# An encoder layer with a routed mixture of experts on one core: its last two experts, its final normalisation and its stores are reordered

## The chip, the cores and the metric

The kernel runs on one core of a Trainium2 chip. The metric is the device time of one execution, in microseconds (us). The engines are TensorE (PE in the profile, its weight loads PEld), VectorE (DVE), ScalarE (ACT), GpSimd (POOL) and SyncE (SP), whose queue issues all the loads and stores here. A small q behind an engine's name in a row (DVEq, SPq) means its sequencer, the part that takes in instructions, register loads, branches and waits.

## The reference

The input x has 256 positions of 2048 values, all float32. One layer adds a gated sum of a spatial-gating branch and a differential-attention branch to x, then adds a mixture of 16 experts, and a last norm follows. The part that the change touches is this:

```python
x = x + hier_moe(rmsnorm(x, norm2_g), ...)   # 16 SwiGLU experts, top 2 per position
out = rmsnorm(x, final_g)                    # x * rsqrt(mean(x*x) + 1e-6) * final_g
```

An expert has w1 and w3 of 2048 x 512 and w2 of 512 x 2048. Each position uses two experts of one group of four.

## The kernel before

The 256 positions are two token tiles t of 128 partitions. The experts are worked off in pairs, each expert with room for 64 positions (`CAP`), so that one pair's 128 positions fill the partitions. Positions beyond the room of 64 are handled at the very end by `rest()` (line 832), under a branch on the largest count (`most`, line 650). In the run that is profiled the branch is not taken.

**First stage of the experts** (lines 750 to 766): four rounds q of four experts. In each of eight steps b a round gathers two blocks of the positions' columns (`gather`, line 679) and multiplies them with four weight blocks of 1 MB (`stream.whole()`, line 57). `swiglu` (line 720) ends a round, and `turn` (line 732) transposes its result one round later. This stage reads 128 blocks.

**Second stage** (lines 807 to 829): for each of four column groups n of 512 and each of eight pairs p, two blocks of w2 (1 MB each) are multiplied into one PSUM bank `ps` (line 817). ScalarE writes the weighted sum's high part `yh` (line 826), VectorE the rest `yl` (line 827), and `back` (line 784) multiplies both with the matrix `PT` that puts the positions back, into the accumulator `ya`, one bank for each token tile (line 792). `back` runs one pair late, so that TensorE has the next pair's blocks in between; only the last call, on line 829, has nothing in between. `yh` and `yl` share a pool of two buffers, so a pair's `yh` waits until `back` has read the last pair's. The second stage reads 64 blocks.

**Final norm.** For n below 3, the last pair's `back` adds x, squares (line 797) and multiplies with the final norm's weights `gf` (`last_norm`, line 775) while the weights of the next n stream in. For n = 3, x is put into `ya` by an identity matmul (line 789); after the last pair ScalarE squares `ya` of both tiles (line 801), then copies it to `xf` (line 803). `last_scale` (line 779) makes the reciprocal root for each tile with a sum and a scaling on VectorE and a power on GpSimd (line 126). Lines 893 and 896 load the branch's register on each engine and branch. After it six instructions scale (lines 905 to 910) and six stores write 2 MB (line 913): columns 0 to 511, 512 to 1535 and 1536 to 2047, each for two tiles.

**What sets the order.** A scheduler puts each engine's instructions in a fixed order when the program is built; `issue_after(i)` holds what a block traces on i's engine behind i. Blocks go into 27 SBUF slots of 1 MB (`Slots`, line 30), of which 17 are free for the stream once the final norm's five are taken (line 770). Loads share eight completion semaphores in turn, so a load is issued only when the eighth before it has landed. `gf` is one load on line 771: it copies the one row of 2048 weights to all 128 partitions, 1 MB in all, and stands in SP's queue behind 17 of the second stage's blocks:

```python
xf, zf, gf = [slots.take()[0] for _ in range(2)], [slots.take()[0] for _ in range(2)], slots.take()[0]
nc.sync.dma_start(gf, rows(A["final_g"], D))            # 128 partitions, step 0
```

Of the kernel before, what the change touches and what calls it, by code (L numbers as in the profile page):

```python
# [22 lines left out]
NE = 16  # L23
CAP = 64
# [72 lines left out]
def encoder(ctx, tc, A, out, stop=None):  # L97
    nc = tc.nc
    V, SC, PE, GP = nc.vector, nc.scalar, nc.tensor, nc.gpsimd

    consts = ctx.enter_context(tc.tile_pool(name="consts", bufs=1))
# [407 lines left out]
    for i in range(4):  # L509
        if i % 2 == 0:  # L510
# [5 lines left out]
            for j in range(4):  # L516
                c = j % 2 * NK + (i + j // 2) * 4
# [16 lines left out]
    for n in range(4):  # L534
# [44 lines left out]
    for n in (0, 2):  # L579
        ps = acc(), acc()  # L580
# [139 lines left out]
    def swiglu(q, s13):  # L720

        out = []
        for p in range(2):
            g = wk(name="g")
            for j in range(2):
                h, ps = slice(j * CAP, (j + 1) * CAP), s13[p][:, j * 512:(j + 1) * 512]
                SC.activation(g[h], ps[:CAP], AF.Silu)  # L727
                V.tensor_tensor(g[h], g[h], ps[CAP:], op=OP.mult)  # L728
            out.append(g)
        return out  # L730

    def turn(q, gated):

        if q % 2 == 0:
            hids.append(slots.take())
        for p in range(2):
            f = bank("f")
            for j in range(4):
                PE.transpose(f[:, j * 128:(j + 1) * 128], gated[p][:, j * 128:(j + 1) * 128], ident)
            SC.copy(view(hids[-1], 4)[:, 2 * (q % 2) + p], f)  # L740

    hids, PTs = [], None
    gathering = gather()
    xg, last, scaled = next(gathering)
    with tc.issue_after(scaled):
        weigh()
    PTs = slots.take(F32R)
    PT = view(PTs, 8)
    gated = None
    for q in range(NE // 4):  # L750
        s13 = acc("s13"), acc("s13")
        for b in range(8):
            with tc.issue_after(last):
                if b == 1 and gated:
                    turn(q - 1, gated)
                xg_next, last, _ = next(gathering, (None, last, None))
            with tc.issue_after(last):
# [12 lines left out]
    xf, zf, gf = [slots.take()[0] for _ in range(2)], [slots.take()[0] for _ in range(2)], slots.take()[0]  # L770
    nc.sync.dma_start(gf, rows(A["final_g"], D))
    sf = consts.tile([128, 2, 4], F32, name="sf")
    rf = consts.tile([128, 2], F32, name="rf")

    def last_norm(n, t):
        c = slice(n * 512, (n + 1) * 512)
        V.tensor_tensor(zf[t][:, c], xf[t][:, c], gf[:, c], op=OP.mult)

    def last_scale(t):
        V.tensor_reduce(rf[:, t:t + 1], sf[:, t], axis=AX, op=OP.add)  # L780
        V.tensor_scalar(rf[:, t:t + 1], rf[:, t:t + 1], 1.0 / D, 1e-6, op0=OP.mult, op1=OP.add)
        rsqrt(rf[:, t:t + 1], rf[:, t:t + 1])

    def back(n, p, ya, ys):

        c = slice(n * 512, (n + 1) * 512)
        if p == 0 and n == 3:
            for t in range(2):
                PE.matmul(ya[:, t], ident, x1_cols(t, n), start=True, stop=False)
        for y in ys:  # L790
            for t in range(2):
                PE.matmul(ya[:, t], PT[:, p, t * 128:(t + 1) * 128], y, start=n < 3 and p == 0 and y is ys[0],  # L792
                          stop=p == NE // 2 - 1 and y is ys[1])
        if p == NE // 2 - 1 and n < 3:
            for t in range(2):
                V.tensor_tensor(xf[t][:, c], ya[:, t], x1_cols(t, n), op=OP.add)
                SC.activation(zf[t][:, c], xf[t][:, c], AF.Square, accum_out=sf[:, t, n:n + 1])
                last_norm(n, t)
        elif p == NE // 2 - 1:
            for t in range(2):  # L800
                SC.activation(xf[t][:, c], ya[:, t], AF.Square, accum_out=sf[:, t, n:n + 1])
            for t in range(2):
                SC.copy(xf[t][:, c], ya[:, t])


    waiting = None
    for n in range(4):
        ya = acc("y").rearrange("p (t n) -> p t n", t=2)
        for p in range(NE // 2):
            ps = bank("ye")  # L810
            with tc.issue_after(mm.ins):
                hid = view(hids[p // 4], 4)[:, p % 4].rearrange("p (k s) -> p k s", k=4)
                for b in range(2):
                    w = stream.whole().rearrange("p (j k n) -> p j k n", j=2, k=2)
                    for k in range(2):
                        for j in range(2):
                            mm = PE.matmul(ps[j * CAP:(j + 1) * CAP], hid[:, b * 2 + k, j * CAP:(j + 1) * CAP], w[:, j, k],  # L817
                                           start=b == 0 and k == 0, stop=b == 1 and k == 1)
# [9 lines left out]
            waiting = n, p, ya, (yh, yl)  # L828
    back(*waiting)


    def rest():
# [57 lines left out]
                        V.tensor_tensor(xf[t][:, c], ps[:, t * 512:(t + 1) * 512], xf[t][:, c], op=OP.add)  # L890

    slots.give(*hids, PTs)
    most_v = nc.values_load(most[0:1, 0:1], min_val=0, max_val=S)
    for t in range(2):
        last_scale(t)
    with tc.If(most_v > CAP):
        rest()
        for t in range(2):
            for n in range(4):
                SC.activation(bank("sq"), xf[t][:, n * 512:(n + 1) * 512], AF.Square, accum_out=sf[:, t, n:n + 1])  # L900
                if n < 3:
                    last_norm(n, t)
            last_scale(t)
    c0, c1, c2 = slice(0, 512), slice(512, 1536), slice(1536, D)
    V.tensor_scalar(zf[0][:, c0], zf[0][:, c0], rf[:, 0:1], None, op0=OP.mult)  # L905
    SC.activation(zf[1][:, c0], zf[1][:, c0], AF.Copy, scale=rf[:, 1:2])
    V.tensor_scalar(zf[0][:, c1], zf[0][:, c1], rf[:, 0:1], None, op0=OP.mult)
    SC.activation(zf[1][:, c1], zf[1][:, c1], AF.Copy, scale=rf[:, 1:2])
    for t in range(2):
        V.scalar_tensor_tensor(zf[t][:, c2], xf[t][:, c2], rf[:, t:t + 1], gf[:, c2], op0=OP.mult, op1=OP.mult)  # L910
    for c in (c0, c1, c2):
        for t in range(2):
            nc.sync.dma_start(out[0, t * 128:(t + 1) * 128, c], zf[t][:, c])

# [46 lines left out]
```

## Time and profile before

| | us |
|---|---|
| median of 3 runs | 1084.84 (1083.54 to 1085.14) |
| the profiled execution | 1083.54 |
| its span in the trace | 1081.6 |
| TensorE busy | 1048.3 (97% of the span) |
| VectorE busy | 510.0 (47%) |
| ScalarE busy | 395.9 (37%) |
| share of the load and store queue, over 16 DMA engines | 76.3% |

TensorE's share is an average over stages with different limits. The matmuls' ends are modelled, and they are pipelined, so a short wait between two of them does not show as idle. In the strip of 40 slices the DMA engines stand at 9 tenths and about 421 GB/s from slice 25 to the last but one, that is in all of the time of the two expert stages but their first few tens of us. All times in the rows are us from the start of the span; the time of an execution has 1.94 us more than its span.

### The profile page before, as it was taken

How to read it: one execution, taken by the hardware profiler on the slowest of the kernel's cores; microseconds unless marked ns; L12 is line 12 of the kernel's file. 1: busy time of each engine (PE TensorE's matmuls, PEld its weight loads, DVE VectorE, ACT ScalarE, POOL GpSimd, SP SyncE). 2: the span in 40 equal slices, each digit the busy share in tenths (PEclk: the TensorE clock that was granted, in tenths of full speed). 3: DMA queues.
4: the chain of work that ended last, by engine and by line, in shares of the span. 5: the costliest groups of instructions: out<-in, count | busy, mean ns of one | idle time of the engine just before them, and what ended most of it. 6: DMA issues, size and time to landing. Idle time of an engine off the chain costs nothing. (4 is left out here: it accounts for less than half of the span.)

```text
span 1081.6 us, 13529 instructions
## 1 busy us (share of the span) xinstructions
PE 1048.3 (97%) x5436; PEld 700.1 (65%) x5436; DVE 510.0 (47%) x745; ACT 395.9 (37%) x554; POOL 9.1 (1%) x16
## 2 busy tenths in 40 slices
PE   7999999999999999999999999999999998999995
PEld 7989988998788888888887743444434432333331
DVE  8775676866778655566655541312313111122121
ACT  7564555555566444444443320211211101111112
POOL 1000000000000000000000000000000000000000
PEclk9999999999999999999999999999999999999997
DMA  9914455455875656556964769999999999999994
GB/s 338 420 61 171 156 197 190 158 209 181 272 265 191 228 192 231 191 203 248 364 254 160 299 269 422 421 421 421 422 421 421 420 421 421 421 422 421 420 421 188
DMA packets 48642, 323.29 MB, mean 299 GB/s; under 512 B 5664, under 2 KB 5824, under 8 KB 11072
## 3 DMA queue, kind: packets, MB, share of 16 engines
q1 hardware_dynamic: 48576, 322.39, 76.3%
q8 instruction: 44, 0.72, 0.3%
q14 instruction: 22, 0.18, 0.0%
HBM read 320.25 MB, written 2.11 MB: 298 GB/s over the span
## 5 line engine op out<-in xcount | busy, mean ns | idle before, releaser
L280 PE MATMUL acc<-slot,slot 128*128 128x512 f32 x1920 | 445.2, 391 | 1.1 <-ACT slot L85 0.6
L280 PEld LDWEIGHTS acc<-slot,slot 128*128 128x128 f32 x1920 | 358.2, 188 | 75.2 <-DVE slot L86 1.0
L86 DVE TENSOR_TENSOR slot<-slot,slot 128x1024 fp32r<-128x1024 f32 (+1 forms) x210 | 253.9, 1211 | 166.0 <-ACT slot L85 165.0
L85 ACT CAST slot<-slot 128x1024 fp32r<-128x1024 f32 (+1 forms) x210 | 218.5, 1042 | 254.1 <-PE acc L280 182.1
L763 PE MATMUL s<-slot,slot 128*64 128x512 f32 x1024 | 228.3, 596 | 3.7 <-DMA slot<-in_w_dram 3.7
L763 PEld LDWEIGHTS s<-slot,slot 128*64 128x64 f32 x1024 | 70.1, 137 | 138.3 <-issue 118.5
L264 PE MATMUL acc<-slot,slot 128*128 128x256 f32 x1152 | 143.5, 286 | 6.0 <-ACT slot L85 5.9
L264 PEld LDWEIGHTS acc<-slot,slot 128*128 128x128 f32 x1152 | 140.8, 193 | 7.0 <-ACT slot L85 6.1
L817 PE MATMUL ye<-slot,slot 128*64 128x512 f32 x512 | 122.6, 604 | 4.7 <-DMA slot<-in_w_dram 3.6
L693 DVE TENSOR_TENSOR slot<-slot,slot 128x256 fp32r<-128x256 f32 x64 | 26.3, 419 | 136.8 <-PE gather L696 122.0
L817 PEld LDWEIGHTS ye<-slot,slot 128*64 128x64 f32 x512 | 31.6, 136 | 79.7 <-issue 39.4
L692 ACT CAST slot<-slot 128x256 fp32r<-128x256 f32 x64 | 25.6, 407 | 153.6 <-PE gather L696 143.6
L827 DVE SCALAR_TENSOR_TENSOR yl<-ye,slot_c,yh 128x512 fp32r<-128x512 f32 x32 | 24.0, 750 | 115.8 <-ACT yh L826 115.8
L826 ACT ACTIVATE yh<-ye,slot_c 128x512 fp32r<-128x512 f32 x32 | 22.0, 688 | 129.1 <-PE y L792 129.1
L696 PEld LDWEIGHTS gather<-slot 128*128 128x128 f32 x256 | 32.9, 189 | 19.8 <-issue 19.5
L700 DVE SCALAR_TENSOR_TENSOR slot<-gather,g,slot 128x256 f32<-128x256 f32 x64 | 27.9, 477 | 27.5 <-PE gather L696 27.3
L696 PE MATMUL gather<-slot 128*128 128x256 f32 x256 | 39.5, 296 | 0.0
L728 DVE TENSOR_TENSOR g<-g,s 64x512 f32<-64x512 f32 x16 | 11.1, 691 | 32.5 <-ACT g L727 32.4
L792 PEld LDWEIGHTS y<-yh,slot 128*128 128x128 f32 x64 | 9.6, 188 | 25.6 <-issue 24.8
L727 ACT ACTIVATE g<-s 64x512 f32<-64x512 f32 x16 | 9.5, 591 | 42.7 <-PE s L763 38.9
L792 PE MATMUL y<-yh,slot 128*128 128x512 f32 x64 | 23.7, 452 | 0.3 <-ACT yh L826 0.3
L792 PE MATMUL y<-yl,slot 128*128 128x512 f32 x64 | 20.2, 397 | 0.1
(191 smaller groups left out, 482.1 us busy)
## 6 DMA issues: line engine op xcount, KB each, us to landing
slot<-in_w_dram SPq DMA_DIRECT2D x192, 1024.0 KB, 19.8
slot<-in_w_in_dram SPq DMA_DIRECT2D x68, 1024.0 KB, 4.9
slot<-in_w_out_dram SPq DMA_DIRECT2D x16, 1024.0 KB, 5.0
slot<-in_w_proj_a_dram SPq DMA_DIRECT2D x8, 1024.0 KB, 4.9
slot<-in_w_proj_b_dram SPq DMA_DIRECT2D x8, 1024.0 KB, 4.8
slot<-in_w_in_dram SPq DMA_DIRECT2D x6, 512.0 KB, 8.1
slot<-in_xT_dram SPq DMA_DIRECT2D x8, 256.0 KB, 7.7
slot<-bias_rows SPq DMA_DIRECT2D x8, 256.0 KB, 6.3
```

The lines of the kernel that those rows point to most:

```text
L85: nc.scalar.copy(h, w)
L86: nc.vector.tensor_tensor(l, w, h.bitcast(F32), op=OP.subtract)
L264: PE.matmul(ps[:, j * S:(j + 1) * S], w[:, j * 128:(j + 1) * 128], v, start=kk == 0 and first and j % 2 == 0, stop=kk == nk - 1 and w is w ...
L280: PE.matmul(ps[:, t * 512:(t + 1) * 512], v[:, t * 128:(t + 1) * 128], w, start=kk == 0 and v is a and w is wh, stop=kk == nb * 4 - 1 and ...
L692: SC.copy(s[:, :, 0], x)
L693: V.tensor_tensor(s[:, :, 1], x, s[:, :, 0].bitcast(F32), op=OP.subtract)
L696: mm = PE.matmul(ps[:, k * S:(k + 1) * S], s[:, t, i], d[:, t], start=k == t == i == 0, stop=k == t == i == 1, skip_group_check=True)
L700: out = V.scalar_tensor_tensor(xg[:, k], ps[:, k * S:(k + 1) * S], g2[:, kk:kk + 1], r_row, op0=OP.mult, op1=OP.mult)
L763: mm = PE.matmul(ps[i * CAP:(i + 1) * CAP], xg[:, k, j * CAP:(j + 1) * CAP], w[:, i, k], start=b == k == 0, stop=b == 7 and k == 1)
L792: PE.matmul(ya[:, t], PT[:, p, t * 128:(t + 1) * 128], y, start=n < 3 and p == 0 and y is ys[0], stop=p == NE // 2 - 1 and y is ys[1])
L817: mm = PE.matmul(ps[j * CAP:(j + 1) * CAP], hid[:, b * 2 + k, j * CAP:(j + 1) * CAP], w[:, j, k], start=b == 0 and k == 0, stop=b == 1 and ...
L827: V.scalar_tensor_tensor(yl, ps, sc, yh.bitcast(F32), op0=OP.mult, op1=OP.subtract)
```

## The change

1. The load of `gf` to 128 partitions is gone. In round q = 3, before step b = 5, a new function `final_rows` takes three slots, loads the row of 8 KB to one partition, and four matmuls with a column of ones copy it to all partitions in PSUM; ScalarE copies the four banks to `gf`.
2. The largest count is copied to `beyond` after round q = 1, and each engine loads the branch's register from it ahead of the second stage.
3. For the last pair of the last column group the w2 matmuls run in two halves of 256 columns with a bank each, and `yh`, `yl` and `back` too.
4. `last_scale` treats both token tiles in one sum, scaling and power.
5. For n = 3 too, `last_norm` now multiplies with `gf` ahead of the branch, reading the accumulator in PSUM, beside ScalarE's copy of it.
6. After the branch VectorE scales tile 0 and ScalarE tile 1, in four pieces of 256, 512, 768 and 512 columns, and eight stores write them.

```diff
@@ swiglu
-                V.tensor_tensor(g[h], g[h], ps[CAP:], op=OP.mult)
+                done = V.tensor_tensor(g[h], g[h], ps[CAP:], op=OP.mult)
+        if q == 1:
+            with tc.issue_after(done.ins):
+                V.tensor_copy(beyond, most)
@@ ahead of the first stage
+    beyond = consts.tile([128, 1], I32, name="beyond")
+    def final_rows():
+        xf.extend(slots.take()[0] for _ in range(2))
+        gf.append(slots.take()[0])
+        row = xf[0][0:1, :]
+        nc.sync.dma_start(row, rows(A["final_g"], D, 1))
+        for n in range(4):
+            c, ps = slice(n * 512, (n + 1) * 512), bank("gf")
+            mm = PE.matmul(ps, ones[0:1, :], row[:, c], start=True, stop=True)
+            SC.copy(gf[0][:, c], ps)
+        return mm.ins
@@ first stage, for b in range(8): with tc.issue_after(last):
+                if q == 3 and b == 5:
+                    last = final_rows()
@@ after the first stage
-    xf, zf, gf = [slots.take()[0] for _ in range(2)], [slots.take()[0] for _ in range(2)], slots.take()[0]
-    nc.sync.dma_start(gf, rows(A["final_g"], D))
+    zf, gf = [slots.take()[0] for _ in range(2)], gf[0]
+    most_v = nc.values_load_multi_w_load_instructions(beyond[0:1, 0:1], min_val=0, max_val=S, bass_reorder=False)[1][0]
-    def last_scale(t):
-        V.tensor_reduce(rf[:, t:t + 1], sf[:, t], axis=AX, op=OP.add)
-        V.tensor_scalar(rf[:, t:t + 1], rf[:, t:t + 1], 1.0 / D, 1e-6, op0=OP.mult, op1=OP.add)
-        rsqrt(rf[:, t:t + 1], rf[:, t:t + 1])
+    def last_scale():
+        V.tensor_reduce(rf, sf, axis=AX, op=OP.add)
+        V.tensor_scalar(rf, rf, 1.0 / D, 1e-6, op0=OP.mult, op1=OP.add)
+        rsqrt(rf, rf)
@@ back, last pair, n = 3
             for t in range(2):
-                SC.activation(xf[t][:, c], ya[:, t], AF.Square, accum_out=sf[:, t, n:n + 1])
-            for t in range(2):
-                SC.copy(xf[t][:, c], ya[:, t])
+                SC.activation(zf[t][:, c], ya[:, t], AF.Square, accum_out=sf[:, t, n:n + 1])
@@ second stage
+                halves = [(ps, slice(0, 512))]
+                if n == 3 and p == NE // 2 - 1:
+                    halves = [(ps[:, :256], slice(0, 256)), (bank("ye")[:, :256], slice(256, 512))]
                 for b in range(2):
                     w = stream.whole().rearrange("p (j k n) -> p j k n", j=2, k=2)
+                    for ph, cy in halves:
...
-            SC.activation(yh, ps, AF.Copy, scale=sc)
-            V.scalar_tensor_tensor(yl, ps, sc, yh.bitcast(F32), op0=OP.mult, op1=OP.subtract)
+            for ph, cy in halves:
+                SC.activation(yh[:, cy], ph, AF.Copy, scale=sc)
+                V.scalar_tensor_tensor(yl[:, cy], ph, sc, yh[:, cy].bitcast(F32), op0=OP.mult, op1=OP.subtract)
+                ys += [(yh[:, cy], cy), (yl[:, cy], cy)]
@@ end
-    most_v = nc.values_load(most[0:1, 0:1], min_val=0, max_val=S)
+    last_scale()
     for t in range(2):
-        last_scale(t)
+        SC.copy(xf[t][:, 1536:], y3[:, t])
+        last_norm(3, t, y3[:, t])
     with tc.If(most_v > CAP):
         rest()
...
-    c0, c1, c2 = slice(0, 512), slice(512, 1536), slice(1536, D)
...
+    chunks = [slice(0, 256), slice(256, 768), slice(768, 1536), slice(1536, D)]
+    for c in chunks:
+        V.tensor_scalar(zf[0][:, c], zf[0][:, c], rf[:, 0:1], None, op0=OP.mult)
+        SC.activation(zf[1][:, c], zf[1][:, c], AF.Copy, scale=rf[:, 1:2])
         for t in range(2):
             nc.sync.dma_start(out[0, t * 128:(t + 1) * 128, c], zf[t][:, c])
```

## Rows read from the trace of the kernel before

**Rows 1.** Busy time by stretches, the line of columns first.

```profile
core 0: us, PE busy (x) PEld busy (x) DVE busy (x) ACT busy (x) POOL busy (x), PEclk, DMA share, GB/s
...
700.00:800.00 100.00, 100.00 (x514) 42.39 (x511) 21.93 (x61) 14.67 (x34) 0.00 (x0) 1.00 1.01 421
...
945.00:950.00 5.00, 2.52 (x13) 0.72 (x14) 0.75 (x1) 0.39 (x1) 0.00 (x0) 1.00 1.02 423
...
1020.00:1063.00 43.00, 42.88 (x178) 15.51 (x176) 8.67 (x13) 7.52 (x13) 0.00 (x0) 1.00 0.98 406
1063.00:1082.00 19.00, 5.61 (x24) 1.98 (x18) 4.32 (x10) 4.68 (x9) 1.10 (x2) 0.70 0.30 113
```

**Rows 2.** DMA issues of the whole run: count, KB each, us to landing.

```profile
slot<-in_w_dram SPq DMA_DIRECT2D x192, 1024.0 KB, 19.8
...
slot<-in_final_g_dram SPq DMA_DIRECT2D x1, 1024.0 KB, 19.8
```

**Rows 3.** SP's timeline from 780 us: start, us, instruction.

```profile
781.60 143.37 SPq L60 DMA_DIRECT2D slot<-in_w_dram  x58
927.14 0.33 SPq L771 DMA_DIRECT2D slot<-in_final_g_dram  x1
929.63 114.78 SPq L60 DMA_DIRECT2D slot<-in_w_dram  x47
```

**Rows 4.** Timeline of all engines, last pairs: start, us, engine.

```profile
1061.24 0.73 PE L792 MATMUL y<-yh,slot 128*128 128x512 f32 x2
...
1062.37 3.65 PE L817 MATMUL ye<-slot,slot 128*64 128x512 f32 x16
...
1065.95 0.73 PE L792 MATMUL y<-yh,slot 128*128 128x512 f32 x2
...
1066.72 0.69 ACT L826 ACTIVATE yh<-ye,slot_c 128x512 fp32r<-128x512 f32 x1 [4.02 <-PE y L792]
1067.44 0.75 DVE L827 SCALAR_TENSOR_TENSOR yl<-ye,slot_c,yh 128x512 fp32r<-128x512 f32 x1 [3.96 <-ACT yh L826]
...
1068.24 0.73 PE L792 MATMUL y<-yl,slot 128*128 128x512 f32 x2
```

**Rows 5.** SP's timeline in the first expert stage, while slots hold it.

```profile
649.81 24.82 SPq L60 DMA_DIRECT2D slot<-in_w_dram  x13
```

**Rows 6.** Groups by line from 895 us on.

```profile
L796 DVE TENSOR_TENSOR slot<-y,slot 128x512 f32<-128x512 f32 x6 | 3.9, 686 | 14.3 <-PE y L792 14.3
...
L789 PE MATMUL y<-slot,ident 128*128 128x512 f32 x4 | 2.0, 618 | 0.0
```

**Rows 7.** Timeline behind the last matmul: squares, powers, copies.

```profile
1069.01 0.60 ACT L801 ACTIVATE slot<-y 128x512 f32<-128x512 f32 x1 [1.61 <-PE y L792]
...
1070.15 1.13 POOL L126 TENSOR_TENSOR rf<-rf,mhalf 128x1 f32<-128x1 f32 x2 [447.46 <-DVE rf L781]
1070.17 1.07 ACT L803 COPY slot<-y 128x512 f32<-128x512 f32 x2
```

**Rows 8.** Sequencer instructions of lines 893 and 896: ns, and when.

```profile
L893 DVEq TENSOR_LOAD <-most x1: 535/535/535, 1070.5 to 1070.5; - x1
...
L896 POOLq EVENT_SEMAPHORE  x1: 17/17/17, 1071.4 to 1071.4; - x1
L896 DVEq EVENT_SEMAPHORE  x1: 21/21/21, 1071.7 to 1071.7; - x1
```

**Rows 9.** Timeline behind the branch: scalings, products, stores.

```profile
1071.90 0.48 DVE L905 TENSOR_SCALAR slot<-slot,rf 128x512 f32<-128x512 f32 x1 [1.25 <-DVEq L896]
1072.31 0.75 DVE L907 TENSOR_SCALAR slot<-slot,rf 128x1024 f32<-128x1024 f32 x1
1072.42 5.24 SPq L913 DMA_DIRECT2D out_dram<-slot  x6
...
1072.97 1.41 DVE L910 SCALAR_TENSOR_TENSOR slot<-slot,rf,slot 128x512 f32<-128x512 f32 x2
```

**Rows 10.** GB/s in 40 slices of 0.23 us, 1072.3 to 1081.6.

```profile
GB/s 35 0 70 0 308 379 335 44 9 9 26 264 370 414 485 370 388 423 370 441 388 458 352 476 335 309 423 405 361 379 379 124 0 0 0 0 0 0 0 0
```

**Rows 11.** Stores' issues on SP: ns min, median, max.

```profile
L913 SPq DMA_DIRECT2D out_dram<-slot x6: 338/664/1557, 1072.4 to 1076.5; - x6
```

More of the change, by code (lines that the diff above doesn't have):

```diff
@@ L744, in encoder @@
     xg, last, scaled = next(gathering)
+    xf, zf, gf = [], [], []
+    def final_rows():
[8 more added lines that the diff above has]
+        return mm.ins
     with tc.issue_after(scaled):
@@ L767, in encoder, with last_norm @@
     slots.give(early, rows_split)
-    xf, zf, gf = [slots.take()[0] for _ in range(2)], [slots.take()[0] for _ in range(2)], slots.take()[0]
-    nc.sync.dma_start(gf, rows(A["final_g"], D))
+    zf, gf = [slots.take()[0] for _ in range(2)], gf[0]
+    most_v = nc.values_load_multi_w_load_instructions(beyond[0:1, 0:1], min_val=0, max_val=S, bass_reorder=False)[1][0]
     sf = consts.tile([128, 2, 4], F32, name="sf")
     rf = consts.tile([128, 2], F32, name="rf")
-    def last_norm(n, t):
-        c = slice(n * 512, (n + 1) * 512)
-        V.tensor_tensor(zf[t][:, c], xf[t][:, c], gf[:, c], op=OP.mult)
-    def last_scale(t):
-        V.tensor_reduce(rf[:, t:t + 1], sf[:, t], axis=AX, op=OP.add)
-        V.tensor_scalar(rf[:, t:t + 1], rf[:, t:t + 1], 1.0 / D, 1e-6, op0=OP.mult, op1=OP.add)
-        rsqrt(rf[:, t:t + 1], rf[:, t:t + 1])
+    def last_norm(n, t, x):
+        V.tensor_tensor(zf[t][:, n * 512:(n + 1) * 512], x, gf[:, n * 512:(n + 1) * 512], op=OP.mult)
+    def last_scale():
+        V.tensor_reduce(rf, sf, axis=AX, op=OP.add)
+        V.tensor_scalar(rf, rf, 1.0 / D, 1e-6, op0=OP.mult, op1=OP.add)
+        rsqrt(rf, rf)
     def back(n, p, ya, ys):
@@ L789, in back @@
                 PE.matmul(ya[:, t], ident, x1_cols(t, n), start=True, stop=False)
-        for y in ys:
+        for i, (y, cy) in enumerate(ys):
             for t in range(2):
-                PE.matmul(ya[:, t], PT[:, p, t * 128:(t + 1) * 128], y, start=n < 3 and p == 0 and y is ys[0],
-                          stop=p == NE // 2 - 1 and y is ys[1])
+                PE.matmul(ya[:, t, cy], PT[:, p, t * 128:(t + 1) * 128], y,
+                          start=n < 3 and p == i == 0, stop=p == NE // 2 - 1 and i == len(ys) - 1)
         if p == NE // 2 - 1 and n < 3:
@@ L797, in back @@
                 SC.activation(zf[t][:, c], xf[t][:, c], AF.Square, accum_out=sf[:, t, n:n + 1])
-                last_norm(n, t)
+                last_norm(n, t, xf[t][:, c])
         elif p == NE // 2 - 1:
             for t in range(2):
-                SC.activation(xf[t][:, c], ya[:, t], AF.Square, accum_out=sf[:, t, n:n + 1])
-            for t in range(2):
-                SC.copy(xf[t][:, c], ya[:, t])
+                SC.activation(zf[t][:, c], ya[:, t], AF.Square, accum_out=sf[:, t, n:n + 1])
     waiting = None
@@ L812, in encoder @@
                 hid = view(hids[p // 4], 4)[:, p % 4].rearrange("p (k s) -> p k s", k=4)
+                halves = [(ps, slice(0, 512))]
+                if n == 3 and p == NE // 2 - 1:
+                    halves = [(ps[:, :256], slice(0, 256)), (bank("ye")[:, :256], slice(256, 512))]
                 for b in range(2):
                     w = stream.whole().rearrange("p (j k n) -> p j k n", j=2, k=2)
[L815 to L818, printed above, removed]
+                    for ph, cy in halves:
+                        for k in range(2):
+                            for j in range(2):
+                                mm = PE.matmul(ph[j * CAP:(j + 1) * CAP], hid[:, b * 2 + k, j * CAP:(j + 1) * CAP],
+                                               w[:, j, k, cy], start=b == 0 and k == 0, stop=b == 1 and k == 1)
             with tc.issue_after(mm.ins):
@@ L825, in encoder @@
             sc = slot_c[:, p:p + 1]
-            SC.activation(yh, ps, AF.Copy, scale=sc)
-            V.scalar_tensor_tensor(yl, ps, sc, yh.bitcast(F32), op0=OP.mult, op1=OP.subtract)
-            waiting = n, p, ya, (yh, yl)
+            ys = []
+            for ph, cy in halves:
+                SC.activation(yh[:, cy], ph, AF.Copy, scale=sc)
+                V.scalar_tensor_tensor(yl[:, cy], ph, sc, yh[:, cy].bitcast(F32), op0=OP.mult, op1=OP.subtract)
+                ys += [(yh[:, cy], cy), (yl[:, cy], cy)]
+            waiting = n, p, ya, ys
     back(*waiting)
+    y3 = ya
     def rest():
@@ L899, in encoder @@
             for n in range(4):
[L900 to L903, printed above, removed]
-    c0, c1, c2 = slice(0, 512), slice(512, 1536), slice(1536, D)
[L905 to L911, printed above, removed]
+                x = xf[t][:, n * 512:(n + 1) * 512]
+                SC.activation(bank("sq"), x, AF.Square, accum_out=sf[:, t, n:n + 1])
+                last_norm(n, t, x)
+        last_scale()
+    chunks = [slice(0, 256), slice(256, 768), slice(768, 1536), slice(1536, D)]
+    for c in chunks:
+        V.tensor_scalar(zf[0][:, c], zf[0][:, c], rf[:, 0:1], None, op0=OP.mult)
+        SC.activation(zf[1][:, c], zf[1][:, c], AF.Copy, scale=rf[:, 1:2])
         for t in range(2):
```

## Prediction

> **What bounds the kernel now.** I read the strip of slices first, then the busy time by stretches, the DMA issues, SP's own timeline, and last the instructions of the final 20 us in order of time.
>
> In both expert stages it is the weight stream. From 700 to 1063 us the DMA engines' share stands at 0.98 to 1.01 and the rate at 421 GB/s, 406 in the last stretch where the stream runs out [rows 1]. TensorE looks as full, but its ends are modelled; what tells is one stretch, 945 to 950, in which it is busy for 2.52 of 5 us while the DMA engines go on at 423 GB/s. In that stretch the stream brings something that TensorE does not want. It is the load of the final norm's rows, 1024 KB like a weight block and 19.8 us from issue to landing like one [rows 2]. It was issued at 927.14 and the next block at 929.63: it takes 2.49 us of the queue, a whole block's place, and all 47 later blocks come that much later [rows 3]. So whatever shortens the stream by a block shortens the kernel by 2.49 us, as long as TensorE can follow.
>
> Can it? Over the last pairs the two blocks' matmuls take from 1062.37 to 1065.95, 3.58 us, and `back` from 1061.24 to 1062.37, 1.13 us [rows 4]: 4.71 us against 4.98 for two blocks of the stream. TensorE has only 0.27 us to spare for each pair, 0.13 for a block. In the first stage, while slots rather than the queue held the loads back (13 issues, 12 steps in 24.5 us), it took a block in 2.04 us [rows 5]: 0.45 to spare. Mark these two, the rival on the slow side rests on them.
>
> From the last landing on, the chain is serial: the last two `back` calls, ScalarE's squares, sum and power, the branch, the scaling, the stores.
>
> **The change part by part.**
>
> *The rows' load.* Removed: one place in the stream, -2.49 us. Added: a load of 8 KB. Its bytes at 421 GB/s are 0.02 us; at worst it holds the queue as a whole block does, 2.49. What limits the stream is bytes, so I take it near the lower end, at +0.1.
>
> *The rows' matmuls.* The two identity matmuls of 512 float32 columns stand as four instructions with 2.0 us busy [rows 6]; four of them make 4.0 us, ScalarE's four copies 2.4, at 0.6 each [rows 7]. The register loads cost each engine some 0.5 us once [rows 8]. All this lies in the streams' shadow: some 29 pairs are left, with 0.27 to spare each, 7.8 us, so TensorE has made it up before the end. I count 0; without that cover it would be +4.5.
>
> Where it stands matters more. The row goes into the slot of block 115 (counted from 0), the newest when step 5 of the fourth round begins, so its load can't go ahead of what frees it. The 17 slots left take blocks 116 to 132 first. In the kernel before, 47 of the 192 blocks came behind the rows' load [rows 3], so 145 ahead of it, the first stage's 128 and 17 more: as many as slots were left. So I expect it behind block 132, landing right after it, and TensorE's four matmuls there as well. If TensorE's fixed order has them earlier, it stands still until then (rival 1).
>
> *The last pair in halves.* Before, 2.29 us pass from ScalarE's start on `yh` (1066.72) to its first square (1069.01) [rows 4, 7]. That start waits for `back` of the pair before, which the halves don't move. Behind it, `yh` (0.69) and `yl` (0.75) come in pieces that overlap: a half costs between half and all of these, I take 0.45 and 0.5. First `yh` half to 1067.17, `yl` halves to 1067.7 and 1068.2, two short matmuls and the way to ScalarE some 0.7: 1068.9, or -0.1. Best is -0.35. The cost is on TensorE: the last block's 8 instructions become 16, which I bound with +0.5.
>
> *One sum and power.* GpSimd's two powers end at 1071.28 (1070.15 and 1.13) [rows 7]; the first ran under the second square, the second decides, and it stays. 0.
>
> *Branch register early, last norm ahead of the branch.* VectorE's register load of 0.54 from 1070.5 stands between its last work and the branch; its step past the branch comes at 1071.7, where GpSimd is past at 1071.4 [rows 8]. So the early register may give at most 0.3. But what takes its place: `last_norm` on the last columns, 0.69 each [rows 6], reads the PSUM bank that ScalarE copies from. ScalarE's two copies run from 1070.17 to 1071.24 [rows 7]. If the readers take turns on a bank, VectorE's first product starts at 1070.8, the second, 0.66 behind, ends at 1072.15, and the branch is passed at 1072.2, 0.46 later than now. If they run side by side, it is -0.3. The nearest rows are `yh` and `yl`, which read one bank: there VectorE starts when ScalarE has ended (1066.72 and 0.69, then 1067.44) [rows 4], though it needs ScalarE's result too. I take the turns: +0.46.
>
> The Trainium skill ("PSUM — Partial Sum Buffer", section "PSUM bank collisions raise a hardware error") says that two engines on one bank and quadrant collide even when both read, and that the compiler puts such accesses one behind the other. By that rule this term is +0.46 and the sum as below; by side-by-side reading the sum would be 0.8 lower. No run here shows it.
>
> *Scaling and stores.* The first scaling of 512 columns took 0.48, of 1024 0.75 [rows 9]; 256 should take 0.35, so the first store goes out 0.13 sooner. Two products of 0.7 [rows 9] leave VectorE's work behind the branch, but ScalarE now has a fourth of tile 1 to scale that it had not: no gain at the last piece. From the first store's issue at 1072.42 to the last bytes at about 1079.7 pass 7.3 us for 2.1 MB. At some 400 GB/s [rows 10] that is 5.2, and 0.8 us of the rest pass before the first bytes; 0.9 us is a hole after the first piece (44, 9, 9 and 26 GB/s in four slices of 0.23 us). One of the six issues held SP for 1557 ns, the shortest for 338 [rows 11]. Eight stores of which none holds SP close the hole: -0.9. Eight at the mean of 0.87 each (5.24 us for six [rows 9]) put the last issue 6.1 us behind the first, in place of 4.1, with less behind it: +0.8. I take -0.2, since bytes bind most of the stretch.
>
> **The sum**: -2.49 + 0.1 + 0 - 0.1 + 0 + 0.46 - 0.13 - 0.2 = -2.4. The profiled execution, 1083.54 (span 1081.6 and 1.94 around it), becomes 1081.1; it was the fastest of three and lies 1.30 under the median, so I forecast a median of 1084.84 - 2.4 = 1082.4. With all ends at their best it is -2.49 + 0.02 - 0.35 - 0.3 - 0.13 - 0.9 = -4.15, with the tail's at their worst (+0.5, +0.46, +0.8, the row's load at 0.3) -0.4.
>
> [...]
>
> **The rivals.**
>
> 1. *TensorE stands behind the row (slower).* Its queue is in order. If the four matmuls are queued where the program writes them, ahead of block 116, it waits until the row lands after block 132: 16 blocks, 40 us. After that it has 12 blocks at 2.04, 64 at 2.36 and 4 us of row matmuls, 179 us, where the stream needs 59 times 2.49 and 2 us, 149. The end comes 30 us late; with the 2.4 gained, about 1112. It decides from some four blocks on: TensorE can make up 12 times 0.45 and 64 times 0.13, 13.7 us, of which the matmuls take 4; a stand of up to 9.8 us costs nothing. Against it: SP's order in the kernel before follows the freeing of slots, so TensorE's order should know the row's landing. 0.07.
> 2. *The end gives it back.* Turns on the bank, eight issues that hold SP, longer matmuls, or a row whose load takes a block's place: a time between -1.4 and +1.8, about 1084.3. For it: the median issue of a store held SP for 664 ns, twice the shortest [rows 11]. Against it: each of these has to come out at its bad end. 0.18.
> 3. *Everything overlaps.* Readers side by side, and no hole in the stores: -3.4 to -4.15, about 1081. 0.13.
>
> **How the numbers follow.** The forecast's case (-1.4 to -3.4) has 0.62. 0.2% of the time, about what a measurement of this kernel can tell from no change, is 2.2 us, close to the forecast itself; I put 0.38 of its 0.62 beyond it. Faster is 0.38 + 0.13 = 0.51, same 0.24 + 0.18 = 0.42, slower 0.07. The range reaches from near the best end (1080.7), 1080.5, to the worst of the forecast's terms (1084.4) and most of rival 2, 1084.6.
>
> **What would show it.** In SP's timeline the weight issues run on at 2.49 with no foreign 1 MB among them, the row's behind block 132; the stretch of TensorE at half work near 947 is gone; the last landing comes 2.3 to 2.5 earlier. The rows' matmuls show one short wait, not tens of us. VectorE passes the branch about 0.4 us later after the last square than now, waiting for ScalarE's copies. The forecast is wrong if the last landing is not 2 us earlier, if the last products run beside the copies, or if the time from the first store to the end moves by over 0.8.

## The result, and the profile after

Five runs of the changed kernel gave a median of 1114.38 us (1113.09 to 1114.96), five of the kernel before 1084.75. The ratio is 1.0273, with a 95% interval of 1.0261 to 1.0284: 29.6 us slower, where 2.4 us faster was forecast. The profiled execution took 1113.09 us, its span 1110.9.

Busy time by stretches of the kernel after, the line of columns first:

```profile
core 0: us, PE busy (x) PEld busy (x) DVE busy (x) ACT busy (x) POOL busy (x), PEclk, DMA share, GB/s
700.00:800.00 100.00, 100.00 (x513) 42.43 (x510) 22.04 (x62) 14.70 (x34) 0.00 (x0) 1.00 1.01 421
875.00:911.00 36.00, 0.47 (x4) 0.00 (x0) 0.00 (x0) 0.00 (x0) 0.00 (x0) 0.54 1.01 421
911.00:919.00 8.00, 7.58 (x10) 2.98 (x11) 0.00 (x0) 2.14 (x4) 0.00 (x0) 0.50 0.11 44
919.00:945.00 26.00, 26.00 (x120) 9.92 (x121) 4.25 (x8) 2.46 (x6) 0.00 (x0) 0.94 0.79 316
...
1060.00:1095.00 35.00, 35.00 (x164) 14.04 (x160) 7.65 (x11) 6.14 (x11) 0.00 (x0) 1.00 0.37 153
```

From 875 to 911 us TensorE is busy for 0.47 of 36 us, while the DMA engines go on at 421 GB/s. Then the picture turns: TensorE is full, and in 911 to 919 the DMA engines stand at 0.11. The hole of 945 to 950 [rows 1] is gone, one fourteen times as long has taken its place. From 919 on TensorE never rests again, and in the last 35 us the DMA share is 0.37: the stream, the limit before, is done early, and TensorE sets the end.

What TensorE stood for, in its own timeline (start, us, instruction, idle time before it and what ended it):

```profile
868.38 7.09 PE L783 MATMUL s<-slot,slot 128*64 128x512 f32 x32
911.42 7.16 PE L759 MATMUL gf<-slot,ones 1*128 1x512 f32 x8 [35.95 <-DMA slot<-in_final_g_dram]
918.51 2.08 PE L696 MATMUL gather<-slot 128*128 128x256 f32 x8
```

The eight instructions are the four row matmuls of `final_rows` (two instructions each). They stand behind block 115, in front of the gather and of block 116, and wait 35.95 us for the row. Block 116 itself had landed at 874.33, so it is the order that kept TensorE from it. SP's timeline shows where the row's load went out, in answer to [rows 3]:

```profile
894.26 0.33 SPq L60 DMA_DIRECT2D slot<-in_w_dram  x1
896.74 0.29 SPq L756 DMA_DIRECT2D slot<-in_final_g_dram  x1
923.39 15.35 SPq L60 DMA_DIRECT2D slot<-in_w_dram  x9
```

The load is the 134th issue, right behind block 132, as forecast. Behind it SP has no free slot for 26.65 us, since TensorE frees none while it stands. This is rival 1 as it was written.

The end of the kernel, ScalarE's and then VectorE's timeline (in answer to [rows 4, 7, 9]), and the stores' issues (in answer to [rows 11]; ns min, median, max):

```profile
1098.15 0.60 ACT L820 ACTIVATE slot<-y 128x512 f32<-128x512 f32 x1 [1.25 <-PE y L811]
...
1099.31 0.59 ACT L921 COPY slot<-y 128x512 f32<-128x512 f32 x1
1100.65 0.59 ACT L921 COPY slot<-y 128x512 f32<-128x512 f32 x1 [0.76 <-DVE slot L796]
1102.11 1.95 ACT L934 ACTIVATE slot<-slot,rf 128x256 f32<-128x256 f32 x3 [0.88 <-DVEq L923]
...
1099.93 0.69 DVE L796 TENSOR_TENSOR slot<-y,slot 128x512 f32<-128x512 f32 x1
1101.27 0.69 DVE L796 TENSOR_TENSOR slot<-y,slot 128x512 f32<-128x512 f32 x1 [0.65 <-ACTq L923]
1102.18 1.28 DVE L933 TENSOR_SCALAR slot<-slot,rf 128x256 f32<-128x256 f32 x3 [0.22 <-DVEq L923]
...
L936 SPq DMA_DIRECT2D out_dram<-slot x8: 343/398/897, 1102.6 to 1106.4; - x8
```

Copies and products go strictly in turn: copy 1099.31, product 1099.93, copy 1100.65, product 1101.27. From the first square to the first scaling pass 3.96 us, before 2.83. No store holds SP for 1.5 us any more.

### The profile page after: what moved, and what is told of

It reads as the page before. It is cut to its first block, busy times and chain, and to the rows that moved or that the text cites. A ratio compares the mean times of both kernels' runs of the same rounds, so it can differ in the third digit from the quotient of the medians.

```text
span 1110.9 us, 13596 instructions
## 1 busy us (share of the span) xinstructions
PE 1050.7 (95%) x5464; PEld 709.3 (64%) x5464; DVE 510.7 (46%) x747; ACT 399.2 (36%) x561; POOL 8.7 (1%) x15
## 5 line engine op out<-in xcount | busy, mean ns | idle before, releaser
L839 PE MATMUL ye<-slot,slot 128*64 128x512 f32 (+1 forms) x528 | 117.7, 585 | 0.0
L839 PEld LDWEIGHTS ye<-slot,slot 128*64 128x64 f32 x528 | 35.4, 136 | 66.4 <-issue 52.7
L851 DVE SCALAR_TENSOR_TENSOR yl<-ye,slot_c,yh 128x512 fp32r<-128x512 f32 (+1 forms) x33 | 24.1, 733 | 108.8 <-ACT yh L850 108.8
L850 ACT ACTIVATE yh<-ye,slot_c 128x512 fp32r<-128x512 f32 (+1 forms) x33 | 22.1, 674 | 120.7 <-PE y L811 120.7
L759 PE MATMUL gf<-slot,ones 1*128 1x512 f32 x8 | 7.2, 1072 | 35.9 <-DMA slot<-in_final_g_dram 35.9
L759 PEld LDWEIGHTS gf<-slot,ones 1*128 1x128 f32 x8 | 2.5, 325 | 39.9 <-issue 39.9
L811 PE MATMUL y<-yh,slot 128*128 128x512 f32 (+1 forms) x66 | 23.8, 442 | 0.1
```

The source lines that it names most:

```text
L811: PE.matmul(ya[:, t, cy], PT[:, p, t * 128:(t + 1) * 128], y, start=n < 3 and p == i == 0, stop=p == NE // 2 - 1 and i == len(ys) - 1)
L839: mm = PE.matmul(ph[j * CAP:(j + 1) * CAP], hid[:, b * 2 + k, j * CAP:(j + 1) * CAP], w[:, j, k, cy], start=b == 0 and k == 0, stop=b == 1 ...
L851: V.scalar_tensor_tensor(yl[:, cy], ph, sc, yh[:, cy].bitcast(F32), op0=OP.mult, op1=OP.subtract)
```

## The experiments

The end of each run was measured in the same pieces from its timelines, in us. "Weights" is from TensorE's start on block 40 of the first expert stage to ScalarE's start on the last pair's `yh`; "gate" from the first square to the first scaling on either engine; "code" is the start of the last 16 KB code load against the first store (explained under the last two experiments). Each row comes from the one trace of its run: "weights" differs by up to 0.9 us between the three runs that are alike up to there (rows spread; spread, old gate; second store on ScalarE).

| run | median, us | weights | `yh` to square | gate | scaling to store | store to end | code |
|---|---|---|---|---|---|---|---|
| before | 1084.75 | 350.78 | 2.29 | 2.83 | 0.58 | 9.20 | +0.47 |
| after | 1114.38 | 380.20 | 2.09 | 3.96 | 0.45 | 8.38 | -0.93 |
| rows one stage later | 1084.49 | 350.40 | 2.09 | 3.96 | 0.45 | 8.38 | -0.69 |
| broadcast load | 1085.16 | 350.56 | 2.09 | 3.96 | 0.45 | 8.38 | -0.92 |
| rows only | 1115.32 | 381.03 | 2.30 | 2.83 | 0.58 | 9.29 | +0.49 |
| rows one step later | 1107.29 | 372.92 | 2.10 | 3.96 | 0.45 | 8.57 | -0.51 |
| no row | 1082.74 | 349.12 | 2.09 | 3.96 | 0.44 | 8.54 | -0.40 |
| rows spread | 1082.46 | 348.51 | 2.10 | 3.96 | 0.44 | 8.86 | -0.45 |
| spread, old gate | 1081.92 | 348.42 | 2.09 | 2.52 | 0.38 | 9.57 | +0.59 |
| rows behind block 129 | 1086.95 | 352.86 | 2.09 | 3.96 | 0.44 | 8.36 | -0.69 |
| second store on ScalarE | 1082.14 | 349.33 | 2.09 | 2.52 | 0.38 | 9.83 | +1.98 |
| eight stores only | 1085.41 | 350.99 | 2.30 | 2.83 | 0.45 | 9.81 | +3.85 |

The first four runs ask where the 29.6 us come from. Theory A is rival 1 of the prediction: TensorE stands behind the row because of the place of the row matmuls in its fixed order. By the theories set against it the loss hangs on something else than that place. These four share 21 runs of the kernel before, median 1084.99.

**The row matmuls one stage later.** The load stays where it is, the four matmuls go behind block 141. The new function `final_rows_out` holds the matmuls and copies that stood in `final_rows`, and no gather is tied behind them any more.

```diff
-                    last = final_rows()
+                    final_rows()
...
                 if n == p == 0:
                     turn(NE // 4 - 1, gated)
+                if n == 0 and p == 6:
+                    final_rows_out(gf)
```

> The whole change, with the row's load in its place but the four row matmuls 26 blocks later in TensorE's order (behind block 141, the second stage's seventh pair). Theory A (TensorE's queue stood behind the row, the matmuls' place alone costs it): no stand, 1084.75 - 2.49 + 0.1 - 0.05 = about 1082.3, within 0.7. Rival B (the row's load itself holds SP or the stream; SP issues nothing for 26.65 us behind it): the hole stays, about 1114. Rival C (the new end of the kernel costs it): about 1114.

1084.49 us, ratio 0.9999 (0.9989 to 1.0008). The stand is gone, and all of the loss with it: theory A. But the time that it gave, 1082.3, is missed by 2.2 us: what the smaller load should have brought didn't come. TensorE's timeline and its granted clock show what came in its place:

```profile
939.38 2.84 PE L762 MATMUL gf<-slot,ones 1*128 1x512 f32 x6
942.15 0.73 PE L813 MATMUL y<-yh,slot 128*128 128x512 f32 x2
942.72 0.63 PE L813 MATMUL y<-yl,slot 128*128 128x512 f32 x2
943.28 1.60 PE L762 MATMUL gf<-slot,ones 1*128 1x512 f32 x2
944.81 6.51 PE L841 MATMUL ye<-slot,slot 128*64 128x512 f32 x16
```

```profile
936.00:943.70 7.70, 7.65 (x27) 2.77 (x24) 0.70 (x2) 2.45 (x4) 0.00 (x0) 1.00 1.01 420
943.80:950.60 6.80, 6.80 (x16) 1.71 (x16) 0.59 (x1) 0.59 (x1) 0.00 (x0) 0.50 1.01 418
950.60:960.00 9.40, 9.40 (x42) 3.47 (x40) 1.84 (x3) 1.74 (x3) 0.00 (x0) 1.00 1.01 422
```

Columns as in the stretches above. TensorE is busy for 7.65 of 7.70 us, most of the last 4 with matmuls that read one row, and then its clock falls from 2.4 to 1.2 GHz for 6.8 us; a pair's 16 matmuls take 6.51 us where they took 3.65 [rows 4]. So the rows cost TensorE 4 us of matmuls and 3.4 (half of 6.8) of clock.

**The old broadcast load, everything else of the change kept.**

```diff
-                if q == 3 and b == 5:
-                    last = final_rows()
...
+    xf, zf, gf = [slots.take()[0] for _ in range(2)], [slots.take()[0] for _ in range(2)], slots.take()[0]
+    nc.sync.dma_start(gf, rows(A["final_g"], D))
```

> The change with the old load of the rows to 128 partitions, where it was before, and no row matmuls: halves, one sum, early register, products ahead of the branch and eight stores stay. Theory A: about 1084.75 - 0.05 = 1084.7, within 0.7, since from yh's last start to the end the changed trace takes 14.83 us and the old one 14.88. Rival B: the same. Rival C: about 1114.

1085.16 us, ratio 1.0001 (0.9992 to 1.001). All pieces of the kernel's end together are worth nothing that this run can tell: in the table they add up to 14.88 us, in the kernel before to 14.90.

**The row part alone, on the kernel before.**

```diff
             with tc.issue_after(last):
+                if q == 3 and b == 5:
+                    last = final_rows()
...
-    nc.sync.dma_start(gf, rows(A["final_g"], D))
```

> The kernel before with the row's load and the row matmuls of the change alone, in the change's place. Theories A and B: 1114.4 within 1. Rival C: about 1082.4.

1115.32 us, ratio 1.0274 (1.0259 to 1.029): the whole loss, without any other part of the change.

**The row matmuls one step later** in TensorE's order, behind block 119, the load where it is.

```diff
                 if q == 3 and b == 5:
-                    last = final_rows()
+                    final_rows()
+                if q == 3 and b == 6:
+                    final_rows_out(gf[0])
```

> The whole change with the row matmuls one step later, behind block 119 in place of block 115; the load keeps its place. Theory A: the stand is 36 less 4 times 2.49, 26 us; with 9 us of row matmuls and cold clock, less the 11.5 that 72 blocks give back and the 2.4 of the stream: +21, about 1106. Rival B: 1114, as the load has not moved.

1107.29 us, ratio 1.0204 (1.0188 to 1.022).

```profile
913.57 7.16 PE L762 MATMUL gf<-slot,ones 1*128 1x512 f32 x8 [27.77 <-DMA slot<-in_final_g_dram]
920.66 2.07 PE L696 MATMUL gather<-slot 128*128 128x256 f32 x8
```

Four blocks' work brought ahead of the wait takes 7.3 us off "weights": the place sets the size, as theory A has it. In this run too no gather is tied behind the row matmuls, and they still stand in front of the next gather and of block 120, 27.77 us ahead of their row.

The next four runs ask why the run one stage later gains nothing. They share 26 runs of before, median 1085.04.

**No row at all.** The kernel with the old broadcast load, but GpSimd writes ones into the tile; neither load nor matmuls.

```diff
-    nc.sync.dma_start(gf, rows(A["final_g"], D))
+    nc.gpsimd.memset(gf, 1.0)
```

> The changed end without any rows of final_g: neither the 1 MB load nor the row and its matmuls, GpSimd writes ones in their place (the multiplication by final_g is left out of the result). It shows what the whole row part can be worth at most. Theory D (TensorE has a little spare, and the row matmuls with the clock that falls behind them used it up in the run one stage later): the weight issues end 2.2 to 2.5 us earlier and so does the kernel, 1082.2 to 1082.8 at a median of 1084.9 of before. Rival E (TensorE paces the last 100 us by itself, whatever the stream does, and the 1 MB load stood beside TensorE's work and cost nothing): within 0.6 us of before.

1082.74 us, ratio 0.9979 (0.997 to 0.9988), 2.3 us (1.66 of it in "weights" in the one trace): the load's place in the stream is worth about what the first term of the sum said, 2.49, and TensorE can use it. Rival E falls.

**One row matmul to a pair**, with the pairs 3 to 6 of the first columns.

```diff
-                if n == 0 and p == 6:
-                    final_rows_out(gf)
+                if n == 0 and 3 <= p <= 6:
+                    final_rows_out(gf, p - 3)
```

> As the run one stage later, but one row matmul (two instructions) with each of the pairs 3 to 6 of the first columns in place of four behind block 141. Theory D: no two row matmuls stand together, the granted clock stays at 2.4 GHz, TensorE pays 3.5 to 4 us for the rows and makes them up at 0.15 us a block in the 50 to 57 blocks left, so the end comes 1.5 to 2.4 us earlier than before: 1082.5 to 1083.4. Rival E: as in the run one stage later, 1084.5. Rival F (a one-row matmul lets the clock fall wherever it stands): four falls of 3.4 us or more, 1088 or above.

1082.46 us, ratio 0.9976 (0.9966 to 0.9986). TensorE's timeline of two of the pairs, and the stretch with all four:

```profile
926.35 1.12 PE L761 MATMUL gf<-slot,ones 1*128 1x512 f32 x2
...
928.53 3.65 PE L840 MATMUL ye<-slot,slot 128*64 128x512 f32 x16
932.11 1.12 PE L761 MATMUL gf<-slot,ones 1*128 1x512 f32 x2
...
934.29 3.65 PE L840 MATMUL ye<-slot,slot 128*64 128x512 f32 x16
```

```profile
924.00:946.00 22.00, 21.98 (x86) 7.71 (x84) 2.25 (x3) 4.95 (x8) 0.00 (x0) 1.00 1.01 421
```

A pair with a row matmul takes 5.76 us (926.35 to 932.11), 1.05 more than the 4.71 of [rows 4], so the four cost 4.2 us. The clock stays at 2.4 GHz (1.00), and the end is as early as without any row. Theory D holds, F falls.

**The same with the old gate**: the products of the last columns behind the branch.

```diff
         SC.copy(xf[t][:, 1536:], y3[:, t])
-        last_norm(3, t, y3[:, t])
...
     for c in chunks:
+        if c is chunks[3]:
+            for t in range(2):
+                V.scalar_tensor_tensor(zf[t][:, c], xf[t][:, c], rf[:, t:t + 1], gf[:, c], op0=OP.mult, op1=OP.mult)
+        else:
+            V.tensor_scalar(zf[0][:, c], zf[0][:, c], rf[:, 0:1], None, op0=OP.mult)
```

> As the run with one row matmul to a pair, and behind the branch the products of the last 512 columns again from the copies, as before the change (ScalarE's copies alone stand ahead of the branch). If the turns that copies and products took on the two banks cost the 1.14 us read from the trace, the step from the first square to the first scaling goes from 4.0 back to 2.7 to 2.9 and the kernel is 0.8 to 1.2 us faster than that run: by theory D 1081.4 to 1082.5, faster than both kernels. If what holds the branch is the register or GpSimd's power, the two runs are equal.

1081.92 us, ratio 0.9967 (0.9954 to 0.998): faster than both kernels. The gate falls from 3.96 to 2.52 us; ScalarE's copies run back to back, and what ends it is GpSimd's step past the branch (POOLq L925), right behind its power:

```profile
1069.12 1.07 ACT L924 COPY slot<-y 128x512 f32<-128x512 f32 x2
1069.71 0.70 POOL L126 TENSOR_TENSOR rf<-rf,mhalf 128x2 f32<-128x2 f32 x1 [446.83 <-DVE rf L801]
1070.49 1.95 ACT L941 ACTIVATE slot<-slot,rf 128x256 f32<-128x256 f32 x3 [0.29 <-POOLq L925]
```

But from the first store to the end pass 9.57 us where it was 8.86, so from `yh` on only 0.8 us are left of the 1.44. The medians of this run and the one before it differ by 0.54, and their intervals overlap; only the profile tells the two apart.

**The row matmuls behind block 129.**

```diff
-                if n == 0 and p == 6:
+                if n == 0 and p == 0:
                     final_rows_out(gf)
```

> As the run one stage later, but the four row matmuls behind block 129. TensorE ends that block at about 910, the row lands at about 917: a stand of some 7 us, with four matmuls and a slow clock behind it. By the prediction's reserve (TensorE makes up 0.13 us for each of the 62 blocks left, 8 us, of which the rows take 4) the end moves by about 3 us to the run one stage later, 1087; by theory D the rows and the clock have used the reserve up already, the whole stand shows, 1090 to 1094. Rival E gives 1092 as well.

1086.95 us, ratio 1.0012 (1.0003 to 1.002). The number is that of the prediction's reserve, but not for the reason given: the row lands earlier than I took it, and the stand is 1.42 us, not 7.

```profile
910.06 1.09 PE L742 MATMUL f<-ident,g 128*128 128x128 f32 x8
912.57 6.27 PE L762 MATMUL gf<-slot,ones 1*128 1x512 f32 x8 [1.42 <-DMA slot<-in_final_g_dram]
918.77 6.12 PE L841 MATMUL ye<-slot,slot 128*64 128x512 f32 x16
```

The rest is again the clock: 1.2 GHz from 913.53 to 923.77, 10.24 us. Here the stand of 1.42 us lies right ahead of the fall, so this run alone can't put the fall down to the row matmuls. It tells something about the reserve all the same. Counted from TensorE's start on block 128, block 132 begins 9.8 us later than in the run without a row (20.24 against 10.45) and the last `yh` 4.2 later (164.26 against 160.04): 5.6 us made up in 59 blocks. In the run one stage later block 145 is 6.6 us behind (48.93 against 42.33) and the last `yh` 1.8 (161.87): 4.8 made up in 46. Both are some 0.10 us a block, the prediction took 0.13.

The last two runs ask what the stores' time hangs on. They share 19 runs of before, median 1085.04. In the kernel before, in the stretch from 1072.6 to 1074.6, DMA queues by kind (packets, MB, share):

```profile
q1 hardware_dynamic: 138, 0.25, 34.7%
q8 instruction: 1, 0.02, 3.6%
```

One packet of 16 KB is a load of instructions. It starts at 1072.89, 0.47 us behind the first store, and SP's second store is held 1.557 us just there [rows 11]. In the run with the old gate the same load starts at 1071.46, and the second store is held 1.59. Where the load comes ahead of the first store ("code" below zero in the table), no store is held over 0.91 us.

**The second store issued by ScalarE.**

```diff
-            nc.sync.dma_start(out[0, t * 128:(t + 1) * 128, c], zf[t][:, c])
+            (nc.scalar if t and c is chunks[0] else nc.sync).dma_start(out[0, t * 128:(t + 1) * 128, c], zf[t][:, c])
```

> As the run with one row matmul to a pair and the old gate, but the second store (tile 1, first 256 columns) is issued by ScalarE in place of SP. In that run a code load of 16 KB ran from 1071.46 for 1.08 us while SP's second store was held 1.59 us. Theory G (the code load is SP's and holds SP's queue behind the first store): SP's next issue is then the second 512 columns and is held by the same load, but ScalarE's store goes out at once; the last issue comes no earlier, the DMA engines have 128 KB more to move in the hole: 0 to 0.3 us gained. Theory H (what holds the second store is the store itself, or its queue, and the code load only falls into the same time): ScalarE is held for 1.6 us, its scalings come that much later, and SP's next store is not held: the time from the first store to the end stays or grows.

1082.14 us, ratio 0.9973 (0.9963 to 0.9983). Neither as expected: SP's second to fourth issues take 0.37 to 0.75 us, and the long hold comes at SP's fifth, 1072.41, 1.583 us. The code load had moved with it, to 1072.14.

```profile
L943 SPq DMA_DIRECT2D out_dram<-slot x7: 348/397/1583, 1070.2 to 1074.6; - x7
...
L943 ACTq DMA_DIRECT2D out_dram<-slot x1: 372/372/372, 1070.3 to 1070.3; - x1
```

From the first store to the end it is 9.83 us, 0.26 more than with SP alone.

**Eight stores, and nothing else, on the kernel before.**

```diff
-    c0, c1, c2 = slice(0, 512), slice(512, 1536), slice(1536, D)
+    c0, c1, c2, c3 = slice(0, 256), slice(256, 768), slice(768, 1536), slice(1536, D)
...
```

> The kernel before with the stores alone changed: four column pieces (256, 512, 768, 512) in place of three, eight stores in place of six. The prediction's term was -0.2 for the stores and -0.13 for the first piece (ends -0.9 and +0.8). Theory G: the hole behind the first store ends when the 16 KB code load has ended, which in the kernel before runs from 1072.89 for 1.17 us, whatever the stores are; the second store stays held for about 1.5 us, the first store goes out 0.1 earlier, and the time from the first square to the end moves by less than 0.3 us. Theory H (smaller pieces close the hole): the second issue takes under 0.6 us and the time from the first store to the end falls from 9.2 to 8.4. In the median both lie within 0.9 us of before.

1085.41 us, ratio 1.0006 (0.9997 to 1.0015). Both expectations missed the place. The second store isn't held; the eighth is, for 1.556 us, at 1077.06, and the code load starts at 1076.69.

```profile
L912 SPq DMA_DIRECT2D out_dram<-slot x8: 342/396/1556, 1072.8 to 1077.1; - x8
```

In every one of the five kernels with a hold of over 1.5 us a code load starts within 0.4 us of the held store, whichever store that is. The ends of the load and of the hold go together too. In six traces (before, rows only, rows one step later, no row, rows spread, and spread with the old gate) the load ends while SP issues the second store, and that issue ends 0.36 to 0.38 us behind the load's end, whether it took 0.47 us in all or 1.69. In the four in which the load has ended before that issue starts (after, rows one stage later, broadcast load, rows behind block 129), it takes 0.37. In the last two runs the hold outlasts the load by 0.9 and 1.0 us. That speaks for theory G's cause, that SP waits for its instructions; no run takes the load away, so it isn't shown beyond that. The load falls in another place in each build.

## Why the prediction was wrong

The mechanism was in the prediction, as rival 1, with a price of 1112 and the chance 0.07. **The step that failed** is in the part on the rows' matmuls: "So I expect it behind block 132, landing right after it, and TensorE's four matmuls there as well." In the sum it is the 0 of the row matmuls, hidden in the streams' shadow; in its place 29.4 us more pass from block 40 to the last `yh` (380.20 against 350.78). The load's place came out to the issue, and the row was there a little sooner than that, by 911.42, where block 132 landed at 914.03. The matmuls' place doesn't follow from the load's: SP's and TensorE's orders are two lists. SP's says when a slot comes free; in TensorE's the row matmuls have their place behind block 115, some sixteen blocks too early. The argument against rival 1, "SP's order in the kernel before follows the freeing of slots, so TensorE's order should know the row's landing", rested on rows of SP alone, on none of TensorE. And the diff spoke against it: `final_rows` hands back the last row matmul as `last`, the next gather is issued behind `last`, and block 116 behind that gather. But the chain is not needed: in the run one step later it is gone, and the row matmuls still stand 27.77 us ahead of their row, in front of the next gather, where the program writes them. So the scheduler put them there without regard to the landing; by what estimate, no run shows.

The price of rival 1 was nearly right. The stand was put at 40 us and is 35.95. From the row's landing to the end it said 179 us; from 911.42 to the last pair's `yh`, 1096.07, pass 184.65. The 5 us between them are the clock, by half the time from 911.42 on: it fell to 1.2 GHz at 877.98, during the stand, and came back at 922.36, so the row matmuls took 7.16 us in place of 4 and block 116 began slow. The Trainium skill ("TensorE: Matmul & The Clock Gate", section "What's actually happening") says that the clock is gated by how busy the array has been, with two levels; in the stand the trace agrees. In the run one stage later the engine was busy for 7.65 of 7.70 us and the clock fell none the less: there the trace doesn't agree, if busy is the profile's busy time.

*The rows' load, -2.49.* Right. From block 130's issue to block 150's the kernel before takes 52.26 us, the spread run 49.68. Without any row the kernel is 2.3 us faster.

*The row's own load, +0.1.* It costs nothing: those 49.68 us are 20 steps of 2.48, with the row's issue among them.

*The row matmuls, 0, hidden.* Right in size (4.2 us for 4.0) and right when they stand one to a pair. Four together aren't hidden, and that cost was not in the sum: the clock. Without a stand, this term alone would have turned the forecast into no change (1084.49).

*The halves, -0.1.* 2.29 to 2.09, -0.20.

*One sum and power, 0.* With the old gate the single power ends 2.44 us behind the first square (1070.41 against 1067.97), in the kernel before 2.27 [rows 7]: +0.17, nearly all of it in the power itself: 0.70 us for both tiles at once, where the two of before took 1.10 together [rows 1], 0.55 each. (The first of the two didn't run under the second square, as the prediction has it, but behind it, from 1070.15 on; the end hung on the second all the same.)

*Early register, products ahead of the branch, +0.46.* +1.13. The turns were right, but I let the second copy run beside the first product, as they read two banks. It waited for it (0.76, ended by VectorE). These waits are for semaphores, so they show the order that was built into the program, in which the accumulators of both tiles are one tile of two banks; what the chip would let run side by side, no run shows. The Trainium skill ("PSUM — Partial Sum Buffer", section "PSUM bank collisions raise a hardware error") has the turns for one bank as a dependency that the compiler's scheduler adds, and this trace shows them. Without the products the gate is 2.52, below the 2.83 of before; by subtraction the register's early load gives 0.48, where the prediction had 0.3 at most, and the later power takes 0.17 of it.

*The first piece, -0.13.* 0.58 to 0.45, -0.13.

*The stores, -0.2.* -0.82, near the best end, but not from the smaller pieces: alone they give +0.61, in a build in which the long hold falls on the last store. In the changed kernel the slow gate let the code load (1101.63 to 1102.90) end before the second store's issue at 1103.01, so that none was held. So +1.13 and -0.82 hang together: in the runs with the gate at 2.52 the hold is back, and the store to end at 9.57 and 9.83. The long hold that I read as a store's own cost goes with a code load.

*The end in all*: -0.20 + 1.13 - 0.13 - 0.82 = -0.02, and with the broadcast load the kernel stands at 1.0001. The forecast had +0.03. That the two agree is luck: the gate was 0.67 worse than forecast and the stores 0.62 better, and the two cancel. (The forecast's worst sum, -0.4, also leaves out the first piece; with its -0.13 it is -0.56.)

*Rival 2 and 3.* Rival 2's first cause, the turns, came, without the rest; rival 3 didn't. *The reserve of 13.7 us* held: 35.95 of stand, 7.16 of row matmuls and 1.9 for the slow gather and block behind them (half of 918.58 to 922.36) make 45.0, of which 29.4 show at the last `yh`. TensorE made up 15.6, and 2.5 of them are the hole at 947 that it no longer had.

## What to carry to other kernels

An engine's fixed order is one list for each engine; that a load goes out late in SP's list says nothing of where its readers stand on TensorE, so look for the first instruction in that list which can't run before the load lands, and count the blocks behind it. Small matmuls that hide in a stream's shadow were best dealt out one at a time here: put together they cost their own time and the clock as well. A gain in the last microseconds is to be measured with the whole tail in place, since the code loads, stores and gates there take each other's slack.

## What the hardware showed unexpectedly

- The granted clock fell to 1.2 GHz in the run one stage later with TensorE at 7.65 of 7.70 us busy, with the seventh of eight instructions that each read one row under way; it fell during the same eight behind block 129 too (10.24 us), but there behind a stand of 1.42 us; with the same eight dealt out two to a pair it stayed at 2.4 GHz. Whether one-row reading or something else of these instructions decides isn't shown.
- It fell without any row matmul too, but not every time. The old load leaves TensorE a stand of about 2.5 us near 948. In the runs with the broadcast load and with eight stores alone (2.50 and 2.52 us) the clock went to 1.2 GHz for 3.41 us shortly behind it, in the kernel before (2.48 us) it stayed at 2.4 GHz.
- All five holds of an SP store of 1.56 to 1.69 us have a 16 KB code load that starts between 0.37 us ahead of the held store's issue and 0.13 us behind it. Where that load starts differs from build to build, from 0.93 us ahead of the first store to 3.85 us behind it. The Trainium skill ("Runtime: NRT & Kernel Launch", section "Instruction fetch mechanics") says that crossing a 16 KiB boundary is mostly hidden and that a taken branch can force a fetch; the size agrees, hidden it was not. Which of the two it is here, no run separates.
